# A one-core hybrid decoder trunk: SBUF slots picked by expected release, and store latency in the emission model

## The chip, the cores and the metric

The kernel runs on one core of one Trainium2 chip. The metric is the device time of one execution in microseconds; for the kernel before there are three timed runs, 1,869.14 to 1,875.14 us with a median of 1,870.52 us, and one profiled execution.

## The reference

One decoder layer over a 2,048 x 1,024 float32 input: a pre-norm mixer whose input projection is split into a causal pooling half and a complex-diagonal state-space half, an output projection with a residual add, a SwiGLU feed-forward block of width 2,816, and a final norm.

```python
def reference(x, ...):
    u = rmsnorm(h, norm_mix) @ w_in
    u_pool, u_ssm = u[..., :D_POOL], u[..., D_POOL:]
    y_pool = pool_mixer(u_pool, w_pool, pool_scale)
    y_ssm = ssm_mixer(u_ssm, lam_re, lam_im, log_dt, b_re, b_im, c_re, c_im, d_skip, w_glu, b_glu)
    h = h + concatenate([y_pool, y_ssm], axis=-1) @ w_out
    h = h + (silu(rmsnorm(h, norm_ffn) @ w_gate) * (rmsnorm(h, norm_ffn) @ w_up)) @ w_down
    return rmsnorm(h, norm_final)
```

## The kernel before

**The work.** Everything is held transposed: features in the 128 partitions, 512 tokens in the free dimension, so 2,048 tokens are four token blocks. A float32 product is made of three matmuls in the chip's fp32r type: each operand is split into a high part (ScalarE casts it, `act(hi, t)`) and a low part (VectorE subtracts the cast from the raw values), and the PE adds hi x hi, hi x lo and lo x hi in one PSUM bank. The stages follow each other: input projection, pooling and state-space work beside it, output projection, gate and up products, down products with the final norm. The gate and up products take the stretch from about 590 to 1,400 us, and every time in the text that falls there belongs to them.

**Gate and up products.** The product is cut into 2 x 2 blocks and made with seven block products instead of eight, named P1, P5, P6, P3, P7, P2, P4 in the order of `PR`. The loop runs over two pairs of token blocks (`hh`) and 11 pairs of feature blocks (`g`), so 22 groups; in each, `matrices` (line 1577) makes the seven products for gate and for up, 12 matmuls each. ScalarE copies some finished banks out to SBUF (line 1613, an eviction), VectorE adds others onto such copies; sigmoid, multiply and the block sums that the down stage will need follow, and `keep_ff` (line 1529) with `put` (line 1443) stores the seven results of a group to DRAM (`act..._P1` and so on), 256 KB each. `w_fetch` and `w_prep` (lines 1314, 1325) load the weights of later groups and split them. All DMAs are issued by SyncE from one queue, in order.

**Slots.** SBUF is cut by hand into slots of three sizes: 2 of 8 KB a partition (names b0, b1), 46 of 4 KB (s0 to s45) and 10 of 2 KB (t0 to t9). `Slots` (line 44) hands out a tag from a queue of free ones, always the one freed longest ago:

```python
        tag = self.free_ids.popleft()
```

`Units` (line 69) hands out 2 KB units. It takes a spare part of a large slot that it has already cut up, if there is one; else a t slot; else it cuts up a b slot into four (while `quads` is set) or an s slot into two:

```python
        if not self.spare[dt]:
            if self.small.left():
                return self.small(shape, dt)
            if self.quads and self.quad.left():
                pool, n = self.quad, 4
```

A slot is freed in the program's text when its last user has been emitted, not when that user has run. The first write to a slot's new tile therefore waits, by a semaphore, for all that still reads or writes the old one, a DMA that stores it included.

**The order of the work.** `Flow` (line 116) is a small model of the machine that runs while the program is written. It keeps a clock `now` for the PE, one each for VectorE, ScalarE, GpSimd and the DMA queue, and for each piece of a slot the time at which it was last written (`wrote`) and read (`read`). Streams of work beside the main one are generators; `poll` takes a step of each when the model's clocks say that its turn has come. So the model's times set the order on VectorE, ScalarE and SyncE, and the chip follows that order with its own times. In `dma` (line 206) a store marks its source as read at the time at which the transfer ends.

Of the kernel before, what the change touches and what calls it, by code (L numbers as in the profile page):

```python
# [29 lines left out]
KE = 8  # L30
MOST, KU, M0, M1, MD = 18, 8, 8, 12, 30
WL, WC = 7, 4
OP, RS = (2, 3), 12
HI, HK0, WPM, HF = (3, 2), 6, 5, 2
WAT, PF, TB, LK, BK = (3, 1), 3, 2, 1, 2
HK = "l"
# [7 lines left out]
class Slots:  # L44


    def __init__(self, pool, tag, n):
        self.pool, self.free_ids, self.of = pool, deque(f"{tag}{i}" for i in range(n)), {}
        self.count = 0

    def __call__(self, shape, dt=F32):
        if not self.free_ids:
            raise RuntimeError("no free slot")
        tag = self.free_ids.popleft()
        self.count += 1
        t = self.pool.tile(shape, dt, tag=tag, name=f"{tag}_{self.count}")
        self.of[id(t)] = (tag, t)
        return t
# [10 lines left out]
class Units:  # L69
# [9 lines left out]
                + (4 * self.quad.left() if self.quads else 0))  # L79

    def __call__(self, shape, dt=F32):
        if not self.spare[dt]:
            if self.small.left():
                return self.small(shape, dt)
            if self.quads and self.quad.left():
                pool, n = self.quad, 4
            elif self.used < self.most:
                pool, n = self.big, 2
                self.used += 1
            else:  # L90
                raise RuntimeError("no free unit")
            t = pool([128, n, 512], dt)
            self.spare[dt] += [(t, i, pool, n) for i in range(n)]
        part = self.spare[dt].pop(0)
        u = part[0][:, part[1], :]
        if len(shape) == 3:
            u = u.rearrange("p (a b) -> p a b", a=shape[1])
        self.of[id(u)] = (u, part, dt)
        return u
# [17 lines left out]
class Flow:  # L117
# [85 lines left out]
    def dma(self, dst, src):  # L203
        self.nc.sync.dma_start(dst, src)  # L204
        n = 4
        for d in dst.shape:
            n *= d
        us, ks = n / 3.5e5, self._keys(dst)
        self.t["d"] = max(self.t["d"], self.now) + us
        t = max([self.now, self.when(src)] + [self.read.get(k, 0.0) for k in ks]) + us  # L210
        self._end(max([t, self.t["d"]] + [self.wrote.get(k, 0.0) - 2.2 for k in ks]), 2.2, dst, [src])

    def read_of(self, ap):
        return max(self.read.get(k, 0.0) for k in self._keys(ap))
# [53 lines left out]
def hybrid_kernel(ctx: ExitStack, tc: tile.TileContext, x4, win, wpl, wglu, wout, wg, wu, wd, vecs, pinv,  # L268
# [6 lines left out]
    B, S = Slots(spool, "b", NB_), Slots(spool, "s", NS_)  # L275
    T = Units(Slots(spool, "t", NT_), S, B)
    PS = Slots(ppool, "p", 8)
    fl = Flow(nc)
    tt, ts, stt, cp, act, mm = fl.tt, fl.ts, fl.stt, fl.cp, fl.act, fl.mm

    def bank():
        return PS([128, 512])
# [683 lines left out]
    def main():  # L966
# [169 lines left out]
        def y_ssm(tb, keep=2):  # L1136
            while ssm[0] in fl.sides:
                yield fl.now + 0.5
            yield from room(2, keep)
            for i in (2, 3):  # L1140
                y_load(tb, i)
            for i in (2, 3):
                yield fl.when(yr[tb, i]) - 0.2
                yield from room(2, keep)
                y_split(tb, i)
            yield max(fl.t["v"], fl.t["a"]) + 0.5
            yield from glu(tb)
# [49 lines left out]
        def w_done(tb, m, ps):  # L1197
            fl.until(lambda: (tb, m // 2) in hin)
            hq = ht[tb, m // 2][:, m % 2, :]
            tt("v", hq, ps, hq, ADD)  # L1200
            PS.free(ps)
            h_sq(tb, m)
# [267 lines left out]
        for tb in range(4):  # L1470
            nxt = []
            for m in range(8):
                if (tb, m) == OP:
                    fl.side(ops_prep(0, 1))
                if tb < 3:
                    if m == 1:
                        nxt.append(fl.side(y_ssm(tb + 1)))
                    elif m == 4:
                        fl.side(h_in(tb + 1))
                elif m == 0:  # L1480
                    for i in range(2):
                        S.free(*gl[i])
                    T.most, res[0] = M0, 0
                elif m == WPM:
                    wp += [fl.side(w_fetch()), fl.side(w_prep())]
                fl.until(lambda: (1, m // 2) in wo)
                ps = bank()
                yield from w_part(tb, m, range(4 if (tb, m) in early else 0, 8), ps)
                w_done(tb, m, ps)
                if tb == 3 and m % 2:  # L1490
                    for half in range(2):
                        S.free(*wo.pop((half, m // 2), ()))
            for i in (2, 3):
                S.free(*yh.pop((tb, i)))
            if tb % 2 and (0, tb // 2) in ph:
                for g in range(4):
                    S.free(*ph.pop((g, tb // 2)))
            fl.side(h_finish(tb), HK if tb > 1 else "v")
            for n in nxt:
                fl.drain(n)  # L1500
# [430 lines left out]
```

## Time and profile before

| what | us |
|---|---|
| median of the three runs | 1,870.52 |
| the profiled execution's own time | 1,865.18 |
| its span, first to last instruction | 1,863.1 |
| PE busy in the span | 1,779.1 (95%) |
| VectorE busy | 1,331.9 (71%) |
| ScalarE busy | 711.6 (38%) |
| 16 DMA engines, the core's own queue | 50.8% of the span |
| mean granted clock of TensorE | 0.982 |

The PE row counts matmuls that overlap in the pipeline, so a busy PE says little of its rate; the number of matmuls in a stretch of fixed length says more. An engine that has less than all its time busy may still hold another one up at single places, and those places are found in the view of waits and in the timeline.

### The profile page before, as it was taken

How to read it: one execution, taken by the hardware profiler on the slowest of the kernel's cores; microseconds unless marked ns; L12 is line 12 of the kernel's file. 1: busy time of each engine (PE TensorE's matmuls, PEld its weight loads, DVE VectorE, ACT ScalarE, POOL GpSimd, SP SyncE). 2: the span in 40 equal slices, each digit the busy share in tenths (PEclk: the TensorE clock that was granted, in tenths of full speed). 3: DMA queues.
4: the chain of work that ended last, by engine and by line, in shares of the span. 5: the costliest groups of instructions: out<-in, count | busy, mean ns of one | idle time of the engine just before them, and what ended most of it. 6: DMA issues, size and time to landing. Idle time of an engine off the chain costs nothing.

```text
span 1863.1 us, 23354 instructions
## 1 busy us (share of the span) xinstructions
PE 1779.1 (95%) x8192; PEld 1453.6 (78%) x8192; DVE 1331.9 (71%) x2385; ACT 711.6 (38%) x1226; POOL 10.9 (1%) x29
## 2 busy tenths in 40 slices
PE   7999989899878899999999999999999999999997
PEld 6887767677767788787788887888778888888886
DVE  7979697657788667775778766777676556675666
ACT  5522333243243333332444333433244444454452
POOL 0000000000000000000000000000000000000000
PEclk9999999999999899999999999999999999999998
DMA  6461442474753444324644454443556666776653
GB/s 189 142 134 59 94 105 80 117 303 180 261 203 140 137 153 159 119 102 153 209 163 141 140 174 168 157 141 132 172 212 238 196 196 188 248 267 183 230 187 113
DMA packets 173093, 311.37 MB, mean 167 GB/s; under 512 B 25712, under 2 KB 52336, under 8 KB 172976
## 3 DMA queue, kind: packets, MB, share of 16 engines
q1 hardware_dynamic: 172976, 309.88, 50.8%
q8 instruction: 64, 1.05, 0.2%
q14 instruction: 53, 0.43, 0.1%
HBM read 210.59 MB, written 98.04 MB: 166 GB/s over the span
## 4 chain that ended last, share of the span: by engine, by line
PE 83%; DVE 7%; DMA 7%; SPq 2%; issue 1%; ACT 1%; DVEq 0%; ACTq 0%
PE p L189 83%; DVE s L166 3%; DMA act_P<-b 2%; SPq L204 2%; DMA act_P<-s 1%; DVE t L166 1%; DVE b L166 1%; DVE s L177 1%; DMA s<-in_win_dram 1%; DMA s<-hp 0%; DMA s<-in_wout_dram 0%; ACT b L185 0%; DMA hp<-s 0%; DMA ys<-b 0%; DMA s<-in_cst_dram 0%
## 5 line engine op out<-in xcount | busy, mean ns | idle before, releaser
L189 PE MATMUL p<-s,s 128*128 128x512 f32 (+3 forms) x5540 | 1386.6, 385 | 50.5 <-ACT s L185 25.2
L189 PEld LDWEIGHTS p<-s,s 128*128 128x128 f32 (+2 forms) x5540 | 989.9, 185 | 273.1 <-ACT s L185 28.2
L189 PE MATMUL p<-s,t 128*128 128x512 f32 (+1 forms) x1548 | 474.7, 387 | 8.7 <-DMA s<-in_wout_dram 4.2
L189 PEld LDWEIGHTS p<-s,t 128*128 128x128 f32 x1548 | 290.0, 190 | 69.5 <-issue 4.6
L166 DVE TENSOR_TENSOR s<-s,s 128x512 f32<-128x512 f32 (+5 forms) x299 | 261.8, 897 | 55.6 <-ACT s L185 36.6
L185 ACT ACTIVATE s<-b 128x512 fp32r<-128x512 f32 (+1 forms) x273 | 167.3, 629 | 229.3 <-PE p L189 166.1
L185 ACT ACTIVATE s<-s 128x512 fp32r<-128x512 f32 (+4 forms) x239 | 175.2, 746 | 144.8 <-DVE s L166 60.5
L166 DVE TENSOR_TENSOR s<-p,s 128x512 f32<-128x512 f32 (+3 forms) x209 | 134.1, 658 | 73.1 <-PE p L189 62.5
L185 ACT ACTIVATE b<-p 128x512 f32<-128x512 f32 (+1 forms) x105 | 61.2, 594 | 244.2 <-PE p L189 113.6
L166 DVE TENSOR_TENSOR s<-b,s 128x512 fp32r<-128x512 f32 (+1 forms) x166 | 113.2, 688 | 57.2 <-issue 30.1
L185 ACT ACTIVATE s<-p 128x512 f32<-128x512 f32 (+2 forms) x121 | 70.0, 591 | 188.5 <-PE p L189 86.2
L189 PE MATMUL p<-t,s 128*128 128x512 f32 (+1 forms) x292 | 108.6, 387 | 0.0
L166 DVE TENSOR_TENSOR t<-b,s 128x512 fp32r<-128x512 f32 (+1 forms) x125 | 85.7, 687 | 11.5 <-issue 4.7
L189 PE MATMUL p<-t,t 128*128 128x512 f32 x196 | 75.6, 389 | 0.0
L166 DVE TENSOR_TENSOR b<-p,b 128x512 f32<-128x512 f32 x94 | 64.6, 688 | 10.7 <-PE p L189 9.1
L166 DVE TENSOR_TENSOR s<-s,t 128x512 f32<-128x512 f32 (+1 forms) x55 | 37.8, 689 | 43.8 <-ACT t L185 26.5
L185 ACT ACTIVATE t<-s 128x512 fp32r<-128x512 f32 (+1 forms) x68 | 42.8, 632 | 68.9 <-DVE s L166 66.3
L166 DVE TENSOR_TENSOR s<-t,s 128x512 fp32r<-128x512 f32 (+2 forms) x71 | 47.7, 674 | 28.4 <-issue 21.9
L166 DVE TENSOR_TENSOR b<-b,b 128x512 f32<-128x512 f32 (+2 forms) x76 | 51.3, 676 | 23.3 <-DMA act_P<-b 12.4
L189 PEld LDWEIGHTS p<-t,s 128*128 128x128 f32 x292 | 54.9, 188 | 11.0
L166 DVE TENSOR_TENSOR s<-s,b 128x512 f32<-128x512 f32 x80 | 55.1, 689 | 11.6 <-DMA act_P<-s 6.4
L185 ACT ACTIVATE t<-b 128x512 fp32r<-128x512 f32 (+1 forms) x78 | 48.9, 627 | 36.4 <-DVE b L166 21.9
(105 smaller groups left out, 1052.5 us busy)
## 6 DMA issues: line engine op xcount, KB each, us to landing
act_P<-b SPq DMA_DIRECT2D x84, 256.0 KB, 5.0
b<-act_P SPq DMA_DIRECT2D x84, 256.0 KB, 3.5
s<-in_x_dram SPq DMA_DIRECT2D x40, 512.0 KB, 6.8
b<-ws_P SPq DMA_DIRECT2D x77, 256.0 KB, 2.8
act_P<-s SPq DMA_DIRECT2D x66, 256.0 KB, 5.1
b<-in_wd_dram SPq DMA_DIRECT2D x62, 256.0 KB, 3.2
t<-act_P SPq DMA_DIRECT2D x53, 256.0 KB, 3.4
s<-in_wu_dram SPq DMA_DIRECT2D x38, 256.0 KB, 3.3
```

Source lines behind the costliest of these rows:

```text
L166: self.eng(e).tensor_tensor(out, a, b, op=op)
L177: self.eng(e).scalar_tensor_tensor(out=out, in0=a, scalar=s, in1=b, op0=op0, op1=op1)
L185: self.nc.scalar.activation(out=out, in_=a, func=func, **kw)
L189: self.nc.tensor.matmul(out, l, r, start=start, stop=stop, skip_group_check=more)
L204: self.nc.sync.dma_start(dst, src)
```

## The change

Three things. `Slots` no longer takes the slot freed longest ago but the free slot for which the model expects the last reader or writer to be done soonest (`soonest`; among slots that are already done, all have the time `now`, and the one freed longest ago is taken). `Units` compares in the same way the spare parts, the t slots, and a large slot to be cut up, for which it adds 1.0 us; on equal times a t slot now comes ahead of a spare part. And a store marks its source as read `DS` = 3.0 us after the transfer's modelled end. The new constant `OK = "v"` is the value that `side` has by default, so that line does nothing.

```diff
--- before.py
+++ after.py
@@ -30,7 +30,8 @@
 KE = 8
 MOST, KU, M0, M1, MD = 18, 8, 8, 12, 30
 WL, WC = 7, 4
-OP, RS = (2, 3), 12
+OK = "v"
+OP, RS, DS = (2, 3), 12, 3.0
 HI, HK0, WPM, HF = (3, 2), 6, 5, 2
 WAT, PF, TB, LK, BK = (3, 1), 3, 2, 1, 2
 HK = "l"
@@ -47,11 +48,17 @@
     def __init__(self, pool, tag, n):
         self.pool, self.free_ids, self.of = pool, deque(f"{tag}{i}" for i in range(n)), {}
         self.count = 0
+        self.ready = lambda tag, chunks: 0.0
+
+    def soonest(self):
+        return min(((self.ready(t, range(4)), i) for i, t in enumerate(self.free_ids)), default=(1e9, 0))
 
     def __call__(self, shape, dt=F32):
         if not self.free_ids:
             raise RuntimeError("no free slot")
-        tag = self.free_ids.popleft()
+        i = self.soonest()[1]
+        tag = self.free_ids[i]
+        del self.free_ids[i]
         self.count += 1
         t = self.pool.tile(shape, dt, tag=tag, name=f"{tag}_{self.count}")
         self.of[id(t)] = (tag, t)
@@ -79,19 +86,22 @@
                 + (4 * self.quad.left() if self.quads else 0))
 
     def __call__(self, shape, dt=F32):
-        if not self.spare[dt]:
-            if self.small.left():
-                return self.small(shape, dt)
-            if self.quads and self.quad.left():
-                pool, n = self.quad, 4
-            elif self.used < self.most:
-                pool, n = self.big, 2
-                self.used += 1
-            else:
-                raise RuntimeError("no free unit")
+        spare = self.spare[dt]
+        old = min(((p[2].ready(p[2].of[id(p[0])][0], (p[1],)), i) for i, p in enumerate(spare)), default=(1e9, 0))
+        pool = self.quad if self.quads and self.quad.left() else self.big if self.used < self.most else None
+        new = pool.soonest()[0] + 1.0 if pool else 1e9
+        few = self.small.soonest()[0]
+        if min(old[0], few, new) == 1e9:
+            raise RuntimeError("no free unit")
+        if few <= min(old[0], new):
+            return self.small(shape, dt)
+        if new < old[0]:
+            n = 4 if pool is self.quad else 2
+            self.used += pool is self.big
             t = pool([128, n, 512], dt)
-            self.spare[dt] += [(t, i, pool, n) for i in range(n)]
-        part = self.spare[dt].pop(0)
+            old = (new, len(spare))
+            spare += [(t, i, pool, n) for i in range(n)]
+        part = spare.pop(old[1])
         u = part[0][:, part[1], :]
         if len(shape) == 3:
             u = u.rearrange("p (a b) -> p a b", a=shape[1])
@@ -208,7 +218,10 @@
         us, ks = n / 3.5e5, self._keys(dst)
         self.t["d"] = max(self.t["d"], self.now) + us
         t = max([self.now, self.when(src)] + [self.read.get(k, 0.0) for k in ks]) + us
-        self._end(max([t, self.t["d"]] + [self.wrote.get(k, 0.0) - 2.2 for k in ks]), 2.2, dst, [src])
+        t = max([t, self.t["d"]] + [self.wrote.get(k, 0.0) - 2.2 for k in ks])
+        self._end(t, 2.2, dst, [])
+        for k in self._keys(src):
+            self.read[k] = max(self.read.get(k, 0.0), t + DS)
 
     def read_of(self, ap):
         return max(self.read.get(k, 0.0) for k in self._keys(ap))
@@ -276,6 +289,8 @@
     T = Units(Slots(spool, "t", NT_), S, B)
     PS = Slots(ppool, "p", 8)
     fl = Flow(nc)
+    B.ready = S.ready = T.small.ready = lambda tag, chunks: max(
+        [fl.now] + [max(fl.read.get((tag, c), 0.0), fl.wrote.get((tag, c), 0.0)) for c in chunks])
     tt, ts, stt, cp, act, mm = fl.tt, fl.ts, fl.stt, fl.cp, fl.act, fl.mm
 
     def bank():
@@ -1471,7 +1486,7 @@
             nxt = []
             for m in range(8):
                 if (tb, m) == OP:
-                    fl.side(ops_prep(0, 1))
+                    fl.side(ops_prep(0, 1), OK)
                 if tb < 3:
                     if m == 1:
                         nxt.append(fl.side(y_ssm(tb + 1)))
```

The order of the matmuls on the PE stays as it was, but for four of them near the end (about 1,820 us) that move ahead of six others. On VectorE and ScalarE neighbours change places by a few rows between 582 and 1,400 us. What changes nearly everywhere is which slot an instruction writes to, and so what it waits for. In the rows below a name has the slot (b1), the number of its tile and a running number; p7 is a PSUM bank. The brackets name the semaphores waited for: DMAHW is a DMA's landing, the others are engines.

ScalarE, the end of the first gate and up group (about 600 to 612 us), before:

```order
L185 ACTIVATE t6_103_4982<-b0_5_4575 128x512 [waits DVE_49]
L185 ACTIVATE b1_7_4764<-p0_192_4971 128x512 [waits DVE_49,PE_49]
L185 ACTIVATE s45_351_4512<-p2_193_4994 128x512 [waits DMAHW1_49,DVE_49,PE_49]
L185 ACTIVATE s41_386_4911<-s19_377_4752 128x512
L185 ACTIVATE b1_7_4764<-p7_194_5014 128x512 [waits DMAHW1_49,DVE_49,PE_49]
```

and now:

```order
L195 ACTIVATE s32_381_4803<-b0_5_4576 128x512 [waits DVE_49]
L195 ACTIVATE t1_104_4993<-p0_192_4971 128x512 [waits PE_49,Activation_49]
L195 ACTIVATE t0_106_5015<-p2_193_4995 128x512 [waits PE_49]
L195 ACTIVATE s32_381_4803<-b1_8_4764 128x512 [waits DVE_49,Activation_49]
L195 ACTIVATE t6_108_5045<-p7_194_5017 128x512 [waits PE_49,Activation_49]
```

The last row is the same eviction, of bank p7. It went to a part of slot b1, behind a store out of it; now it goes to t6, whose last tile was an operand of matmuls, and no DMA semaphore is left in its wait. The eviction of p2 two rows above it has moved in the same way from s45 to t0.

ScalarE, the seventh group (about 845 to 853 us), before:

```order
L185 ACTIVATE s2_391_5157<-s30_406_6569 128x512 [waits DVE_49,PE_49]
L185 ACTIVATE s38_399_5840<-p0_228_6648 128x512 [waits DMAHW0_49,DVE_49,PE_49]
L185 ACTIVATE s13_393_5407<-s33_402_6180 128x512
L185 ACTIVATE b1_7_4764<-p2_229_6684 128x512 [waits DMAHW1_49,DVE_49,PE_49]
L185 ACTIVATE s30_406_6569<-p7_230_6703 128x512 [waits DMAHW7_49,DVE_49,PE_49]
```

and now:

```order
L195 ACTIVATE s24_437_6764<-p2_229_6744 128x512 [waits PE_49]
L195 ACTIVATE s0_432_6575<-s6_428_6483 128x512 [waits DVE_49]
L195 ACTIVATE t1_216_6781<-t2_209_6571 128x512 [waits DMAHW6_49]
L195 ACTIVATE s33_440_6792<-b0_5_4576 128x512 [waits DMAHW7_49]
L195 ACTIVATE t4_218_6796<-p7_230_6766 128x512 [waits PE_49]
```

The eviction of bank p7 in the last row went to slot s30 behind a store, and now goes to t4 and waits for the PE alone. Of the rows ahead of it some casts have changed places.

SyncE, the loads near 740 us, before:

```order
L204 DMA bsP7_1_3566<-t9_151_5836 128x512 [waits DMAHW0_49,DVE_49]
L204 DMA bsP4_1_3568<-s38_399_5840 128x512 [waits DMAHW1_49,DVE_49]
L204 DMA t6_161_6113<-in_wg_dram 128x512 [waits DMAHW2_49,Activation_49]
L204 DMA t9_162_6115<-in_wu_dram 128x512 [waits DMAHW3_49,DMAHW0_49]
L204 DMA s38_399_5840<-bn2_1_124 128x512 [waits DMAHW4_49,DVE_49]
L204 DMA t2_164_6122<-bn3_1_128 128x512 [waits DMAHW5_49,PE_49]
L204 DMA t1_165_6124<-bn3_3_130 128x512 [waits DMAHW6_49,PE_49]
```

and now:

```order
L214 DMA t1_175_6005<-in_wg_dram 128x512 [waits DMAHW0_49,PE_49]
L214 DMA s4_413_5887<-in_wu_dram 128x512 [waits DMAHW3_49,DMAHW1_49]
L214 DMA t3_183_6153<-in_wg_dram 128x512 [waits DMAHW2_49,DVE_49,PE_49]
L214 DMA b0_5_4576<-in_wu_dram 128x512 [waits DVE_49]
L214 DMA s4_413_5887<-bn2_1_124 128x512 [waits DMAHW4_49,DVE_49]
L214 DMA s0_419_6161<-bn3_1_128 128x512 [waits DMAHW5_49]
L214 DMA s0_419_6161<-bn3_3_130 128x512 [waits DMAHW6_49]
```

The third row is the same weight load. It went to t6, which waited for ScalarE, and now goes to t3, which waits for VectorE and the PE; the row behind it waits for VectorE, and the loads of the normed activations (bn) follow.

## Rows read from the trace of the kernel before

**Rows 1.** The page's first line: the span.

```profile
span 1863.1 us, 23354 instructions
```

**Rows 2.** The chain that ended last, share of the span by line (page, part 4).

```profile
PE p L189 83%; DVE s L166 3%; DMA act_P<-b 2%; SPq L204 2%; DMA act_P<-s 1%; DVE t L166 1%; DVE b L166 1%; DVE s L177 1%; DMA s<-in_win_dram 1%; DMA s<-hp 0%; DMA s<-in_wout_dram 0%; ACT b L185 0%; DMA hp<-s 0%; DMA ys<-b 0%; DMA s<-in_cst_dram 0%
```

**Rows 3.** Windows of 50 us: busy time (instructions) by engine, PEclk, DMA share, GB/s.

```profile
600.00:650.00 50.00, 43.74 (x181) 35.58 (x180) 30.73 (x49) 16.27 (x29) 0.00 (x0) 0.90 0.39 128
650.00:700.00 50.00, 50.00 (x222) 41.42 (x221) 32.04 (x52) 18.52 (x34) 0.00 (x0) 1.00 0.50 165
...
750.00:800.00 50.00, 47.38 (x203) 38.72 (x202) 36.62 (x60) 17.07 (x30) 0.00 (x0) 0.97 0.39 129
...
850.00:900.00 50.00, 45.74 (x193) 36.71 (x192) 32.19 (x52) 18.15 (x34) 0.00 (x0) 0.97 0.48 163
...
1150.00:1200.00 50.00, 49.14 (x217) 40.38 (x216) 31.08 (x50) 15.12 (x27) 0.00 (x0) 1.00 0.58 195
1200.00:1250.00 50.00, 49.15 (x218) 40.35 (x217) 35.92 (x58) 19.73 (x36) 0.00 (x0) 1.00 0.45 152
...
1300.00:1350.00 50.00, 48.53 (x215) 39.86 (x214) 31.09 (x51) 14.26 (x25) 0.00 (x0) 1.00 0.51 167
1350.00:1400.00 50.00, 48.46 (x213) 39.54 (x212) 34.11 (x54) 20.28 (x36) 0.00 (x0) 1.00 0.60 215
```

**Rows 4.** Waits, 590 to 1,400 us: us in total, times, longest.

```profile
ACT b L185 <- DMA act_P<-b: 97.0, 18, 10.4
DVE b L166 <- DMA act_P<-b: 81.3, 20, 6.5
ACT s L185 <- DVE b L166: 70.2, 43, 6.8
...
ACT s L185 <- DMA act_P<-s: 52.2, 9, 8.1
...
PE p L189 <- ACT s L185: 11.3, 4, 6.3
...
PE p L189 <- ACT b L185: 6.5, 4, 2.6
```

**Rows 5.** Waits of the PE, 200 to 590 us.

```profile
PE p L189 <- DVE s L166: 18.5, 9, 4.6
PE p L189 <- DVE b L166: 7.4, 3, 3.7
```

**Rows 6.** Timeline, 599 to 613 us: start, us, engine, line, op, [idle before <-releaser].

```profile
599.99 0.69 DVE L166 TENSOR_TENSOR t<-b,s 128x512 f32<-128x512 f32 x1
...
605.88 0.39 PE L189 MATMUL p<-s,t 128*128 128x512 f32 x1
...
606.03 0.42 SPq L204 DMA_DIRECT2D act_P<-b  x1
...
611.35 0.60 ACT L185 ACTIVATE b<-p 128x512 f32<-128x512 f32 x1 [9.97 <-DMA act_P<-b]
...
612.52 0.79 PE L189 MATMUL p<-s,s 128*128 128x512 f32 x1 [6.26 <-ACT s L185]
```

**Rows 7.** DMA issues (page, part 6): times, KB each, median us to landing.

```profile
act_P<-b SPq DMA_DIRECT2D x84, 256.0 KB, 5.0
...
act_P<-s SPq DMA_DIRECT2D x66, 256.0 KB, 5.1
...
s<-in_wu_dram SPq DMA_DIRECT2D x38, 256.0 KB, 3.3
```

**Rows 8.** Timeline near 740 us: a weight load, a matmul group, the casts of that weight.

```profile
740.91 0.38 SPq L204 DMA_DIRECT2D t<-in_wg_dram  x1
...
753.98 0.84 PE L189 MATMUL p<-s,s 128*128 128x512 f32 x3
...
776.34 1.14 ACT L185 ACTIVATE s<-t 128x512 fp32r<-128x512 f32 x2
```

**Rows 9.** The down stage as one window, columns as in rows 3.

```profile
1400.00:1850.00 450.00, 447.48 (x2038) 372.26 (x2036) 286.70 (x506) 203.12 (x355) 1.79 (x3) 1.00 0.63 206
```

## The prediction

> **What bounds the kernel now.** The chain of work that ended last lies on the PE for 83% of the span [rows 1, 2]. Behind it come stores to the buffers of the gate and up products (act_P, 2% and 1%), each about as long in the chain as VectorE's largest line. A store ends nothing by itself, so it can stand in such a chain only where somebody waits for the memory it reads from. I then read the windows of 50 us. The PE is busy nearly all the time in each, but the number of matmuls tells its rate: a window that runs undisturbed has 222, and of the sixteen from 600 to 1,400 us seven have clearly fewer [rows 3]. The down stage behind is busy for 447.48 of 450 us [rows 9], so it has little to give.
>
> Next the waits. From 590 to 1,400 us the PE waits for ScalarE alone, 11.3 and 6.5 us in eight places, and ScalarE waits 97.0 and 52.2 us for the landing of stores [rows 4]. The two are one chain, and the timeline of the longest place shows it [rows 6]. VectorE has read the old contents of a slot by 600.68 us (599.99 + 0.69). The store out of that slot is issued only at 606.03 us, behind other DMAs in SyncE's queue. ScalarE, which is to evict a finished bank into the same slot, starts at 611.35 us after 9.97 us idle. Behind it stands the cast that the PE needs. The PE, whose last matmul began at 605.88 us, goes on at 612.52 us after 6.26 us idle.
>
> Before 590 us the PE waits mostly for VectorE's results, 18.5 and 7.4 us [rows 5]. Those are operands not yet made, with VectorE at work until the moment it delivers them; no store and no slot stands behind them.
>
> **The change, part by part.**
>
> *Slots picked by expected release.* The change adds and removes no instruction. It moves the evictions at the eight places away from slots behind a fresh store. At the first place the eviction of bank p7 now goes to t6, and in the seventh group to t4: both slots held operands of matmuls, the ScalarE rows have no DMA semaphore left in their wait, and the bank itself is finished by those same or later matmuls. So the new wait costs nothing: the eviction has to wait for that bank anyhow. The others of the eight go the same way: seven now go to slots that matmuls read last, and one to a slot whose store landed some 40 us earlier. I carried the same check over all instructions of the stretch: with the end times of the trace before, no ScalarE or VectorE instruction of the changed order waits for a recent store. What goes is therefore all of ScalarE's 97.0 and 52.2 us and VectorE's 81.3 us [rows 4], nearly all of it idle time that cost nothing, and with it the eight waits of the PE.
>
> What the eight are worth I take from the windows, since a pause also leaves the clock at its lower level (1.2 instead of 2.4 GHz) for a while: PEclk is 0.90 and twice 0.97 where the longest pauses lie, and 1.00 elsewhere [rows 3]. The windows with 181, 203, 193, 217, 218, 215 and 213 matmuls lack 41, 19, 29, 5, 4, 7 and 9 against 222: 114 in all. At 50 / 222 = 0.225 us each that is **25.7 us**. The waits alone make 11.3 + 6.5 = 17.8 us [rows 4]; the remaining 7.9 us are matmuls at the lower clock and the restart after each pause. So 17.8 us is the lower bound if the clock comes back no better, and 25.7 us the value I take, because the clock rows show the loss in the same windows as the pauses.
>
> Would the next limit stand right behind? At the first place ScalarE was free from 601.4 us and the PE asked at about 606.3 us, so some 5 us lie between, and the operands that follow are made by engines that are idle today: VectorE is busy 30.73 of 50 us there, ScalarE 16.27 [rows 3].
>
> *The store's latency.* The model used to call a store's source free when the transfer ends, 256 KB / 3.5e5 = 0.75 us after its start. Now it adds 3.0 us, 3.75 in all. The trace has 5.0 and 5.1 us from issue to landing [rows 7], so the model is still about 1.3 us short. If each of the eight evictions took a slot at that edge, 8 x 1.3 = 10.4 us would come back; none does, so I take zero. The Trainium skill (DMA: Bandwidth & Descriptors, Anatomy of one DMA) gives a fixed 2.0 us plus bytes at 436e3 per us. By that an estimate for 256 KB is 2.6 us, the model would count too much, and the sum would be the same 25.7 us. The rows differ from that page, and they decide.
>
> *Order and units.* The shifts by a few rows on VectorE and ScalarE add waits of ScalarE for VectorE's last read of a slot. Such waits are today 70.2 us in 43 places without the PE noticing [rows 4], and VectorE, freed of its own 81.3 us, will be earlier. I take zero; the bounds are a gain of nothing and a loss as large as one place of the eight, 25.7 / 8 = 3.2 us.
>
> *SyncE's queue.* Some weight loads now go to slots that matmuls still read. The load issued at 740.91 us would wait in its new slot t3 for a matmul group that ends at about 754.1 us, 13 us later, with the loads and stores behind it in the queue. Its casts run at 776.34 us [rows 8]. A load takes 3.3 us [rows 7], so 754.1 + 3.3 leaves 19 us: zero.
>
> *The sum.* 1,865.2 - 25.7 = **1,839.5 us** for the profiled execution. The median of the runs before is 1,870.52, which is 5.3 us above the profiled one. I carry this over and predict **1,845 us** for the median.
>
> **The rivals.**
>
> *The latency is still counted too short.* Then slots are handed out 1.3 us before the store lands, and 10.4 us come back: 1,845 + 10.4 = 1,855 us. The 5.0 us of the rows speak for it, the absent DMA semaphores in the evictions against. 12%.
>
> *There are too few slots, whichever is picked.* Every slot is then behind some store or reader, the waits only change their names, and the time stays at 1,870 us. This is also the case in which the change does not do what it says. The Trainium skill (Perfetto Trace Analysis, Optimization Strategy) reads the same gap repeated on the engine that should be saturated as a sign that SBUF may be too small for the next tile. The trace agrees as to the gap: it comes back in seven windows [rows 3]. Against the rest of it speaks that the evictions do find slots without a store. 4%.
>
> *The head of SyncE's queue.* All DMAs stand in one queue, so a load that waits for a matmul holds up the stores and loads behind it. It decides when such a load is more than 32 us late (776.3 - 740.9 - 3.3): then the cast waits, ScalarE works in order, and the evictions behind the cast leave the PE without a bank. One such stall costs what one of the eight does, 3.2 us; with one in each of 22 groups, 70 us, and the time is 1,845 + 70 = 1,915 us. From the tenth stall on it is slower than before. For it: the wait of 13 us above. Against: the 19 us that are left. 4%.
>
> **How the numbers follow.** Forecast 80%, the rivals 12, 4 and 4%. A measurement of this kernel can tell about 0.3%, 5.6 us, from no change. Forecast and first rival lie below 1,865, so faster has 0.92, the same 0.04 and slower 0.04. The range goes from 1,838 us (the 1,839.5 of the profiled execution, should the 5.3 us above it not come back, and a little more) to 1,855 us (the first rival; the lower bound of 17.8 us, which gives 1,853, lies inside).
>
> **What would show it.** Right: in the profile after, ScalarE and VectorE have hardly a wait for act_P from 590 to 1,400 us, the PE's waits of 17.8 us there are nearly gone, all sixteen windows have 213 or more matmuls and most 220 to 223, PEclk is 1.00 in them, and the stretch before 590 us looks as it did. The latency rival would show as waits for act_P of 1 to 2 us; the second as waits of old length under other names; the third as casts that wait for weight loads and long waits at the head of SyncE's queue. The prediction is wrong if the gate and up windows are full and the total still stays above 1,855 us, because then the time has gone to another stage.

## The result, and the profile after

The changed kernel takes 1,839.26 us (median; 1,837.82 to 1,842.11 us). The kernel before, run beside it, takes 1,869.94 us (1,869.14 to 1,875.14 us). The ratio is 0.9832, with a 95% interval of 0.981 to 0.9854. Four executions among the comparisons of this study (one of the kernel before, three of edited kernels) took 3,569 to 6,312 us, about twice to three and a half times the rest, and are left out of all ratios and counts. The prediction was 1,845 us with a range of 1,838 to 1,855 us, so the direction and the range hold; the point lies 5.7 us too high, and the result is near the lower end of the range.

The head of the page of the changed kernel, to be read beside [rows 1] and [rows 2]:

```profile
span 1837.1 us, 23226 instructions
...
PE 1770.6 (96%) x8192; PEld 1450.0 (79%) x8192; DVE 1341.1 (73%) x2385; ACT 717.7 (39%) x1226; POOL 10.9 (1%) x29
...
PE 91%; DVE 5%; DMA 2%; SPq 1%; issue 1%; ACT 0%; DVEq 0%; ACTq 0%
PE p L199 91%; DVE s L176 3%; SPq L214 1%; DVE s L187 1%; DMA s<-in_win_dram 1%; DVE t L176 1%; DMA s<-in_wout_dram 0%; DMA s<-in_cst_dram 0%; DMA ys<-b 0%; DMA s<-ys 0%; PE p L203 0%; DVE nwt L176 0%; DVE b L176 0%; ACT s L195 0%; ACT t L195 0%
```

The span is 26.0 us shorter, with the same work (every engine has the same number of working instructions as before; the 128 fewer in the total are others, such as waits). The stores of the gate and up products have left the chain of work that ended last; the PE is 91% of it, 83% before. (All line numbers of the helpers are 10 higher than before: line 199 is the matmul, 195 ScalarE, 176 VectorE, 214 the DMAs.)

Windows of 50 us of the changed kernel, columns as in [rows 3]:

```profile
600.00:650.00 50.00, 50.00 (x223) 41.39 (x222) 39.18 (x64) 22.57 (x41) 0.00 (x0) 1.00 0.55 195
...
750.00:800.00 50.00, 50.00 (x222) 41.42 (x221) 33.93 (x54) 19.50 (x35) 0.00 (x0) 1.00 0.51 177
...
850.00:900.00 50.00, 50.00 (x223) 41.39 (x221) 38.77 (x61) 17.65 (x31) 0.00 (x0) 1.00 0.42 143
...
1350.00:1400.00 50.00, 50.00 (x222) 41.41 (x221) 34.03 (x55) 19.89 (x36) 0.00 (x0) 1.00 0.44 156
```

These are four of sixteen; each of the sixteen has 222 or 223 matmuls and a PEclk (the granted share of TensorE's full clock) of 1.00. In the windows where the kernel before had 181, 203, 193 and 213, nothing is missing any more. The stretch from 600 to 1,400 us as one window gives the best measure of the gain. The PE's columns (us, PE busy, matmuls, PEclk, DMA share, GB/s), of the kernel before:

```profile
600.00:1400.00 800.00, 782.13 (x3411) 0.99 0.46 155
```

and of the changed kernel:

```profile
600.00:1400.00 800.00, 800.00 (x3531) 1.00 0.46 162
```

A matmul of an undisturbed stretch takes 800 / 3,531 = 0.2266 us. The 120 that were missing make 120 x 0.2266 = 27.2 us. That is the whole gain and a little more: the PE's last pause ahead of this stretch, with 2,631 matmuls ahead of it in both traces, now ends at 577.79 us, before at 576.11 us, so the profiled execution after is 1.7 us late there. It falls behind in the first 200 us. The kernel before:

```profile
0.00:200.00 200.00, 188.46 (x931) 1.00 0.48 131
```

and the changed kernel:

```profile
0.00:200.00 200.00, 187.89 (x924) 0.99 0.48 130
```

This is no effect of the change: the second trace of the same changed kernel (the change again, below) has 930 matmuls there, and all the traces of this study have 914 to 931, with a granted clock of 0.98 to 1.00.

Waits from 590 to 1,400 us in the changed kernel (us in total, times, longest), a choice of lines:

```profile
ACT t L195 <- PE p L199: 155.0, 100, 3.5
...
DVE t L176 <- DMA act_P<-t: 4.9, 4, 2.1
ACT b L195 <- DMA b<-act_P: 4.8, 1, 4.8
...
ACT t L195 <- DMA act_P<-t: 0.8, 1, 0.8
```

The PE has no row at all in this view; before, it had 17.8 us [rows 4]. ScalarE's 97.0 and 52.2 us behind stores are 0.8 us now, VectorE's 81.3 us are 4.9 us. A line of the kernel before that the prediction didn't count, VectorE behind stores out of 4 KB slots, has gone as well:

```profile
DVE s L166 <- DMA act_P<-s: 19.7, 5, 5.1
```

ScalarE still idles a lot, but now for the PE to finish a bank, which is what an engine that isn't the bound should wait for. The timeline at the first place, of the changed kernel (start, us, engine, line, operation, idle before):

```profile
602.64 0.60 ACT L195 ACTIVATE t<-p 128x512 f32<-128x512 f32 x1 [1.66 <-PE p L199]
...
604.88 0.39 PE L199 MATMUL p<-s,t 128*128 128x512 f32 x1
...
605.11 2.88 PE L199 MATMUL p<-s,s 128*128 128x512 f32 x12
...
607.83 2.88 PE L199 MATMUL p<-s,t 128*128 128x512 f32 x12
```

This is the eviction of bank p7 that started at 611.35 us after 9.97 us behind a store [rows 6]. It goes to t6 now, starts at 602.64 us, and has waited only for the bank. The PE runs through the place where it stood for 6.26 us.

The PE's waits in the stretch before are nearly the same. Waits of the PE from 200 to 590 us, of the changed kernel, to be read beside [rows 5]:

```profile
PE p L199 <- DVE s L176: 20.1, 11, 4.5
PE p L199 <- DVE b L176: 7.4, 3, 3.7
```

### The profile page after: what moved, and what is told of

Same layout as the page of the kernel before. It is cut to its first block, busy times and chain, and to the rows that moved or that the text cites. A ratio compares the mean times of both kernels' runs of the same rounds, so it can differ in the third digit from the quotient of the medians.

```text
span 1837.1 us, 23226 instructions
## 1 busy us (share of the span) xinstructions
PE 1770.6 (96%) x8192; PEld 1450.0 (79%) x8192; DVE 1341.1 (73%) x2385; ACT 717.7 (39%) x1226; POOL 10.9 (1%) x29
## 4 chain that ended last, share of the span: by engine, by line
PE 91%; DVE 5%; DMA 2%; SPq 1%; issue 1%; ACT 0%; DVEq 0%; ACTq 0%
PE p L199 91%; DVE s L176 3%; SPq L214 1%; DVE s L187 1%; DMA s<-in_win_dram 1%; DVE t L176 1%; DMA s<-in_wout_dram 0%; DMA s<-in_cst_dram 0%; DMA ys<-b 0%; DMA s<-ys 0%; PE p L203 0%; DVE nwt L176 0%; DVE b L176 0%; ACT s L195 0%; ACT t L195 0%
## 5 line engine op out<-in xcount | busy, mean ns | idle before, releaser
L199 PE MATMUL p<-s,s 128*128 128x512 f32 (+4 forms) x4736 | 1188.7, 385 | 37.9 <-DVE s L176 21.8
L199 PEld LDWEIGHTS p<-s,s 128*128 128x128 f32 (+2 forms) x4736 | 840.5, 185 | 227.6 <-DVE s L176 25.5
L199 PE MATMUL p<-s,b 128*128 128x512 f32 x1000 | 319.6, 392 | 7.4 <-DVE b L176 7.4
L199 PEld LDWEIGHTS p<-s,b 128*128 128x128 f32 x1000 | 188.6, 189 | 47.8 <-DVE b L176 8.7
L195 ACT ACTIVATE s<-t 128x512 fp32r<-128x512 f32 (+1 forms) x174 | 105.3, 624 | 113.3 <-PE p L199 76.7
L195 ACT ACTIVATE t<-s 128x512 fp32r<-128x512 f32 (+2 forms) x129 | 78.5, 616 | 163.9 <-DVE s L176 148.6
L199 PE MATMUL p<-b,s 128*128 128x512 f32 (+2 forms) x476 | 132.6, 390 | 4.1 <-DMA s<-s 4.1
L176 DVE TENSOR_TENSOR t<-p,t 128x512 f32<-128x512 f32 x130 | 88.6, 689 | 39.5 <-PE p L199 35.8
L199 PEld LDWEIGHTS p<-b,s 128*128 128x128 f32 (+1 forms) x476 | 73.9, 176 | 25.7 <-issue 9.8
L176 DVE TENSOR_TENSOR t<-t,t 128x512 f32<-128x512 f32 (+2 forms) x121 | 81.7, 675 | 7.9 <-ACT t L195 6.5
```

The costliest lines, as they stand in the source:

```text
L176: self.eng(e).tensor_tensor(out, a, b, op=op)
L195: self.nc.scalar.activation(out=out, in_=a, func=func, **kw)
L199: self.nc.tensor.matmul(out, l, r, start=start, stop=stop, skip_group_check=more)
```

## The experiments

Eleven kernels. The first four and the complement (units alone) take the change apart; one moves the latency the other way; one runs the change again; two take slots away; two eat into the margin of SyncE's queue. All are edits of the changed kernel unless it says otherwise. The table has the profiled execution's time, the ratio to the kernel before on the same chip, and the matmuls from 600 to 1,400 us. "Worked out" is 1,838.88 us (the profiled execution of the change) plus 0.2266 us for each matmul short of 3,531.

| kernel | us | ratio (95%) | matmuls | worked out |
|---|---|---|---|---|
| before | 1,865.18 | 1 | 3,411 | 1,866.1 |
| the change | 1,838.88 | 0.9832 (0.981 to 0.9854) | 3,531 | 1,838.9 |
| no latency | 1,842.46 | 0.9857 (0.9833 to 0.988) | 3,524 | 1,840.5 |
| latency only | 1,870.01 | 1.0008 (0.9993 to 1.0022) | 3,408 | 1,866.8 |
| preference only | 1,884.49 | 1.009 (1.0072 to 1.0107) | 3,333 | 1,883.7 |
| old order of units | 1,873.07 | 1.0025 (1.0013 to 1.0037) | 3,387 | 1,871.5 |
| latency of 6 us | 1,841.27 | 0.9855 (0.9825 to 0.9885) | 3,531 | 1,838.9 |
| eight t slots | 1,840.52 | 0.9854 (0.9837 to 0.9872) | 3,531 | 1,838.9 |
| units alone | 1,839.67 | 0.985 (0.9829 to 0.987) | 3,532 | 1,838.7 |
| the change again | 1,839.77 | 0.9855 (0.9838 to 0.9873) | 3,531 | 1,838.9 |
| loads later | 1,839.91 | 0.9835 (0.9816 to 0.9854) | 3,531 | 1,838.9 |
| loads latest | 1,863.10 | 0.997 (0.9956 to 0.9984) | 3,435 | 1,860.6 |
| less room | 1,863.78 | 0.9953 (0.9939 to 0.9967) | 3,480 | 1,850.4 |

In all rows but the last the two times agree within 4 us: most of what these kernels differ by in time lies from 600 to 1,400 us.

**No latency.**

```diff
-OP, RS, DS = (2, 3), 12, 3.0
+OP, RS, DS = (2, 3), 12, 0.0
```

> The changed kernel with DS = 0: slots are picked by expected release, but a store's source counts as free when the modelled transfer ends, 0.75 us after its start. My theory (what cost time was evictions put into slots whose store was still far from landing, and any choice by release avoids most of that): with the end times of the changed kernel's trace carried over the new order, ScalarE has nine waits for a store of more than 1 us between 590 and 1,400 us, the longest 4.2 us, where the kernel before has more than twenty with several of 6 to 9 us. At the longest place of before, ScalarE's idle time of 9.97 us became 6.26 us at the PE, so some 3.7 us were spare there: waits of up to 4.2 us cost the PE nearly nothing. So 1,839 to 1,844 us. Rival (the latency is what does it, without it the choice is blind to stores): the time goes back to 1,860 us or more. Third theory (both matter about equally): about 1,850 to 1,855 us.

As my theory had it. The PE has one wait left in the stretch, at the first place. Its timeline in this kernel:

```profile
607.00 0.69 DVE L176 TENSOR_TENSOR t<-t,t 128x512 f32<-128x512 f32 x1 [4.21 <-DMA act_P<-t]
...
608.35 1.88 PE L199 MATMUL p<-s,s 128*128 128x512 f32 x7 [1.48 <-DVE s L176]
```

So a slot with a fresh store is picked here, VectorE waits 4.21 us for it, and 1.48 us of that reach the PE; the window lacks seven matmuls, 1.6 us. That is all that the latency is worth in this stretch. Whether it is worth it in the total can't be told: the intervals of this kernel and of the change overlap.

**Latency only** (edits of the kernel before).

```diff
-        self._end(max([t, self.t["d"]] + [self.wrote.get(k, 0.0) - 2.2 for k in ks]), 2.2, dst, [src])
+        t = max([t, self.t["d"]] + [self.wrote.get(k, 0.0) - 2.2 for k in ks])
+        self._end(t, 2.2, dst, [])
+        for k in self._keys(src):
+            self.read[k] = max(self.read.get(k, 0.0), t + DS)
```

> The kernel before with the store's latency alone (the source of a store counts as read 3.0 us after the modelled transfer), slots still handed out in the order in which they were freed. My theory: the choice is blind to the model's times, so evictions go on landing in slots behind fresh stores (carried over, ScalarE has some 30 waits for a store of more than 1 us, ten of them over 5 us); the time stays at 1,864 to 1,876 us, and the windows from 600 to 1,400 us keep a loss of some 100 matmuls. Rival (the latency moves the order of ScalarE's and VectorE's work, since streams wait for reads in the model, and that order is the gain): 1,840 us.

No difference from the kernel before. Waits of ScalarE and VectorE from 590 to 1,400 us in this kernel:

```profile
ACT b L185 <- DMA act_P<-b: 71.7, 12, 11.0
...
DVE b L166 <- DMA act_P<-b: 55.6, 13, 7.4
ACT s L185 <- DMA act_P<-s: 54.6, 15, 6.5
```

The model knows of the stores now, but the queue of free slots doesn't ask it. The order on ScalarE and VectorE does move, and gains nothing by it.

**Preference only.**

```diff
-    B.ready = S.ready = T.small.ready = lambda tag, chunks: max(
-        [fl.now] + [max(fl.read.get((tag, c), 0.0), fl.wrote.get((tag, c), 0.0)) for c in chunks])
```

> The changed kernel with all expected releases read as zero: what stays is the new order of preference in the units (a t slot ahead of a spare part of a large slot) and the latency. My theory: without the times the t slots go to evictions and store results in the order in which they were freed, and waits for stores come back (carried over: 25 of ScalarE over 1 us, 15 of them over 5 us); 1,862 to 1,880 us. Rival (the gain is that evictions now take t slots in place of parts of the two big slots, whatever the time of release): 1,839 to 1,845 us.

Slower than before, and 3.8 us above the upper end I gave (median 1,883.79 us). Waits from 590 to 1,400 us in this kernel:

```profile
DVE t L176 <- DMA act_P<-t: 135.9, 34, 10.8
ACT t L195 <- DMA act_P<-t: 57.2, 15, 9.0
```

and the timeline of its longest pause in the middle of the stretch:

```profile
995.38 0.42 SPq L214 DMA_DIRECT2D act_P<-t  x1
...
1001.32 0.69 DVE L176 TENSOR_TENSOR t<-b,t 128x512 fp32r<-128x512 f32 x1 [7.61 <-DMA act_P<-t]
...
1002.07 1.22 PE L199 MATMUL p<-s,t 128*128 128x512 f32 x2 [6.04 <-DVE t L176]
```

Ten t slots that are always taken first come round quickly, so they come round behind their own stores. The last such store ahead of the wait is the one issued at 995.38 us. What is held up here is a low part that VectorE is to write, and VectorE's results hold the PE for 23.7 of its 28.9 us of waits in the stretch. My count had looked at ScalarE alone, which is likely why it was too small.

**Old order of units.** The choice in `Units` as before, `Slots` and the latency as changed:

```diff
-        spare = self.spare[dt]
-        old = min(((p[2].ready(p[2].of[id(p[0])][0], (p[1],)), i) for i, p in enumerate(spare)), default=(1e9, 0))
...
+        if not self.spare[dt]:
+            if self.small.left():
+                return self.small(shape, dt)
...
+        part = self.spare[dt].pop(0)
```

> The changed kernel with the choice in the units as before (spare part first, then a t slot, then a large slot cut up), while the slots of each size are still picked by expected release and the latency counts. My theory: at seven of the eight places of the kernel before the eviction went to a spare part of a large slot, and a spare part freed behind a store is taken first here as well, so the waits stay (carried over: 31 of ScalarE over 1 us, 14 of them over 5 us): 1,862 to 1,885 us. Rival (the choice among slots of one size is enough): 1,839 to 1,845 us.

The gain is gone. The timeline of the first place in this kernel (its helpers' lines are three lower than in the changed kernel, 192 ScalarE and 196 the matmul):

```profile
615.82 0.60 ACT L192 ACTIVATE b<-p 128x512 f32<-128x512 f32 x1 [10.90 <-DMA act_P<-b]
...
616.99 1.22 PE L196 MATMUL p<-s,t 128*128 128x512 f32 x2 [7.68 <-ACT t L192]
```

It is the picture of [rows 6] once more, 1.4 us longer at the PE: an eviction into a part of a large slot behind that slot's store.

**Units alone.** The complement: slots of 8 and 4 KB in the order of freeing, only the units choose.

```diff
+        l = list(self.free_ids)[:1] if self.tag in "bs" else self.free_ids
-        return min(((self.ready(t, range(4)), i) for i, t in enumerate(self.free_ids)), default=(1e9, 0))
+        return min(((self.ready(t, range(4)), i) for i, t in enumerate(l)), default=(1e9, 0))
```

> The changed kernel with the slots of 8 KB and 4 KB handed out in the order of freeing again; the choice by release stays among the t slots and between t slots, spare parts and large slots. It is the complement of the run with the old order of the units. My theory: the evictions that held the PE up take units, so the whole gain lies in the choice of units; the order of work on every engine is that of the changed kernel, and carried over ScalarE has two waits for stores, 1.4 us in all: 1,836 to 1,844 us. Rival (the choice among large slots carries part of it): 1,848 us or more.

The whole gain. With the run before this one it settles which part of the change works: the choice in `Units` by the expected release, among spare parts, t slots and a new large slot. The choice among slots of one large size did nothing here. Whether the comparison between the kinds is needed, or a choice among the spare parts alone would do, isn't separated: the old order took both away.

**Latency of 6 us.**

```diff
-OP, RS, DS = (2, 3), 12, 3.0
+OP, RS, DS = (2, 3), 12, 6.0
```

> The changed kernel with DS = 6.0 in place of 3.0, so that the model's 6.75 us from the start of a store lie above every median of landing in the trace of before (5.0 and 5.1 us). My theory: the choice with 3.0 avoids the stores already, all windows from 600 to 1,400 us have 222 or 223 matmuls, and there is nothing left to gain: the same as the changed kernel, 1,836 to 1,843 us. Rival (the latency is still counted short and costs somewhere): faster than the changed kernel by 3 us or more.

No gain: the stretch is full at 3.0 already.

**The change again**, with no edit.

> The changed kernel once more, for a comparison on the same chip with the others of this group and for the term of 5.3 us that the prediction carried over from the runs of before. If the profiled execution of before was a fast one by chance, the median here lies within 2 us of the profiled execution, as in the first runs (1,839.26 against 1,838.88 us): 1,836 to 1,843 us. Rival (kernels of this kind take about 5 us more without the profiler): median 1,843 us or more, 4 to 6 us above the profiled execution.

The median is 1,839.77 us and the profiled execution took the same. This kernel has no surcharge on runs beside the profiled one.

**Eight t slots.**

```diff
-NB_, NS_, NT_ = 2, 46, 10
+NB_, NS_, NT_ = 2, 46, 8
```

> The changed kernel with eight t slots in place of ten. It tells how much room the choice needs. My theory: slots without a fresh store are plentiful, so the choice still finds one (carried over, ScalarE has no wait for a store of more than 0.7 us): 1,837 to 1,846 us. Rival (the slots are just enough, and the gain hangs on having ten): waits for stores or readers come back under other names, 1,850 us or more.

As fast as with ten.

**Less room.**

```diff
-NB_, NS_, NT_ = 2, 46, 10
+NB_, NS_, NT_ = 2, 42, 8
```

> The changed kernel with 42 slots of 4 KB in place of 46 and eight t slots in place of ten, 20 KB a partition less. Where the run with eight t slots takes away units alone, this one takes room from every stage; the order on the PE moves too (454 matmuls, all by at most 64 places). My theory: the choice still finds slots without a fresh store from 600 to 1,400 us (carried over, five waits of ScalarE for a store of over 1 us, the longest 3.5 us), but with fewer free slots the evictions wait more for readers, and the input side of the kernel, where I have checked nothing, may lose some too: 1,838 to 1,856 us. Rival (room was scarce all the time, and the choice by release only helped as long as it had 56 slots): 1,860 us or more.

The median is 1,859.33 us, 3.3 us above my range and just short of the rival's. Against the change its profiled execution takes 24.9 us more. The matmuls from 600 to 1,400 us explain 51 x 0.2266 = 11.6 us of it. The rest lies earlier. The window from 400 to 600 us of the PE in this kernel,

```profile
400.00:600.00 200.00, 172.86 (x727) 0.94 0.57 208
```

and in the changed kernel:

```profile
400.00:600.00 200.00, 176.62 (x755) 0.94 0.55 200
```

That is 28 matmuls or 6.3 us less, and from 0 to 400 us another 32 are missing (1,942 against 1,974), 7.3 us. Part of that is scatter: the other kernels with all the slots of the change and its choice have 1,964 to 1,974 matmuls up to 400 us. The PE's waits from 590 to 1,400 us in the kernel with less room name VectorE alone:

```profile
PE p L199 <- DVE s L176: 6.7, 5, 2.3
PE p L199 <- DVE b L176: 1.2, 2, 1.0
PE p L199 <- DVE t L176: 0.9, 1, 0.9
```

VectorE itself waits only 6.9 us for the products' stores there, little more than the 4.9 us of the change. Half of the 51 matmuls are missing in the first window:

```profile
600.00:650.00 50.00, 47.59 (x197) 0.95 0.27 97
```

Three more windows lack 4, 16 and 7 against 222 (from 850 to 950 and from 1,300 to 1,350 us), the others are full, and nothing more is lost after 1,400 us, since the losses up to there (11.6, 6.3 and 7.3 us) already make up the 24.9 us. So a kernel with 50 of these slots loses time that one with 54 doesn't, up to about 650 us and at a few places behind, and what the PE waits for in the stretch are operands that VectorE delivers later. What makes VectorE later there wasn't traced further, and the order on the PE moved too, so room and order aren't separated.

**Loads later.**

```diff
-WL, WC = 7, 4
+WL, WC = 4, 4
```

> The changed kernel with the weights loaded at most 4 products ahead in place of 7 (WL = 4). In the changed kernel the DMA at the head of SyncE's queue waits 210.7 us in 28 places for matmuls between 590 and 1,400 us, 21.1 us the longest, against 20.2 us in 16 places before; the prediction gave a load about 32 us until its cast is late, 19 us of them left at the place it looked at. A product takes about 36.8 / 7 = 5.3 us (22 groups in 810 us), so loads come some 16 us later. My theory (the queue has that margin): 3 us of the 19 are left, at most a few short pauses: 1,838 to 1,850 us. Rival (the waits at the head of the queue have used the margin up): casts wait for loads in most of the 22 groups, 3.2 us each, up to 1,839 + 70 = 1,909 us.

No loss: no wait of the PE in the stretch, 3,531 matmuls. The loads do come later: by the trace they are issued 16 us (median) further on in the PE's work than in the changed kernel.

**Loads latest.** The same line with `WL = 2`.

> The same with WL = 2: loads come 5 products or 26 us later than in the changed kernel, more than the 19 us that were left at the place of the prediction, but less than the 32 us from a load's start to its cast. My theory: now the casts are late by some 7 us and pauses come back; with 3.2 us in each of 22 groups up to 70 us, 1,860 to 1,910 us. Rival (even 26 us less does not matter): 1,845 us or less. Third theory (the third rival of the prediction was priced too low): above 1,910 us.

The median is 1,863.75 us, inside my range, but the mechanism is not the one I had described. The loads are issued 28 us (median) further on in the PE's work, and yet ScalarE waits only 2.1 us for a weight load in the stretch. What has gone is the lead of the work on the weights: `w_prep` can't cast a weight before `w_fetch` has emitted its load, so `WL = 2` also holds the casts below the four products that `WC` allows. Some waits of ScalarE for the products' stores are back as well. Waits from 590 to 1,400 us in this kernel:

```profile
PE p L199 <- DVE b L176: 4.1, 7, 1.7
PE p L199 <- ACT t L195: 2.5, 4, 1.2
...
ACT t L195 <- DMA act_P<-t: 17.7, 12, 2.5
```

A place in the timeline of this kernel:

```profile
1231.74 0.63 ACT L195 ACTIVATE t<-t 128x512 fp32r<-128x512 f32 x1 [2.17 <-DMA act_P<-t]
...
1232.41 0.69 DVE L176 TENSOR_TENSOR b<-t,t 128x512 fp32r<-128x512 f32 x1 [2.61 <-ACT t L195]
...
1232.43 0.73 PE L199 MATMUL p<-s,t 128*128 128x512 f32 x2 [0.77 <-ACT t L195]
```

Cast, low part and matmul start within 0.7 us of each other, so a small delay, here a cast that stood behind a store for 2.17 us, reaches the PE. How much of the loss is the lost lead and how much the stores wasn't separated. Two windows of the PE in this kernel show the result:

```profile
1200.00:1250.00 50.00, 49.09 (x214) 1.00 0.38 132
...
1350.00:1400.00 50.00, 48.55 (x209) 1.00 0.60 221
```

All sixteen windows lack some matmuls, 2 to 13 of 222, and the granted clock stays at 1.00. This is a thin loss everywhere, where the kernel before had eight pauses.

## Why the prediction was right, and where it was off

*What bounds the kernel, and the eight places.* Right. The eight pauses are gone, and with them ScalarE's and VectorE's waits for the products' stores. The experiments show the cause: wherever evictions and low parts go to slots behind fresh stores (latency only, preference only, old order of units), 123 to 198 matmuls are missing, and where the choice in `Units` avoids most of that, none or seven, unless room or the lead of the loads is cut far down.

*The price, 25.7 us.* Right for the profiled executions: 1,865.18 - 1,838.88 = 26.3 us. The one long window gives 27.2 us: an undisturbed window has 222 or 223 matmuls, 222.4 in the mean of the sixteen after the change, and I had counted all against 222. That the forecast for the profiled execution came within 0.6 us is partly luck, because the 1.5 us by which the price is short of 27.2 us are about the 1.7 us that the execution after was late by its first 200 us. The lower bound of 17.8 us (the PE's waits alone) was 9 us short. So the pauses did cost about half as much again as they lasted, as the windows' matmuls said. Where the extra half lies can be read from [rows 3]: the three windows with a granted clock of 0.90 and 0.97 lack 89 matmuls, 20.0 us, while the PE is idle for 13.1 us; the four with 1.00 lack 25, 5.6 us, with 4.7 us idle. So nearly all of it is in the windows where the clock fell.

*The carry-over of 5.3 us.* This step failed, and it is the only one that moved the number. I took the distance between the profiled execution before and the median for a property of the kernel that the change would keep. Over all comparisons of this study the kernel before has 52 times with a median of 1,868.0 us, from 1,860.9 to 1,875.1 us; 6 of them lie at or below the profiled 1,865.18 us. The changed kernel has eight, from 1,837.8 to 1,842.1 us. The profiled execution before was a low draw from a wide scatter, the one after an ordinary one from a narrow one. Eight times say little of how narrow, though: 26 executions of seven kernels without long pauses (the change twice, no latency, latency of 6 us, eight t slots, units alone, loads later) go from 1,835.5 to 1,843.5 us. Nor does the scatter belong to the pauses alone: loads latest, which has no long pause, spreads over 8.3 us in ten executions, and latency only, which has them, over 8.0 us in ten. It does go with the granted clock. Of the 48 executions before for which the mean clock is on record, the five with 0.983 took 1,860.9 to 1,865.9 us, the three with 0.978 took 1,871.5 to 1,874.5 us. A part lies outside the gate and up stretch: the profiled execution before had 931 matmuls in its first 200 us, the most of any trace here. What makes the clock differ between executions stays open.

*The latency.* Right that 3.0 us suffices, wrong in the weight I gave it. The first rival priced a latency that is 1.3 us short at 10.4 us. With no latency at all only seven matmuls are missing, 1.6 us, and with 6.0 us none are gained. A likely reason, not tried by itself, lies in the rule: among the slots that the model takes for done, the one freed longest ago comes first, so one whose store is still under way is seldom next.

*Too few slots.* This rival did not come true, and two t slots less cost nothing. Six slots less do cost some 20 us, but VectorE's and ScalarE's waits for the products' stores stay at 6.9 and 4.2 us there, so it isn't the rival as I had described it. The sign that the Trainium skill names (Perfetto Trace Analysis, Optimization Strategy: the same gap coming back can mean that there isn't enough SBUF for the next tile) was there in the trace before. Here the slots were enough, and the handing out was wrong.

*SyncE's queue.* The cost of zero was right and the wait that I had found was not a single one. The DMA at the head of the queue waits for matmuls, from 590 to 1,400 us in the changed kernel,

```profile
SPq L214 <- PE p L199: 210.7, 28, 21.1
```

and in the kernel before:

```profile
SPq L204 <- PE p L189: 20.2, 16, 5.1
```

Ten times as much, up to 21.1 us where I had worked out 13. But the head of the queue doesn't wait longer in all: every row of that view together makes 588 us before and 590 us now, because the waits for VectorE fell from 510 to 361 us. Loads that come some 16 us later still cost nothing, and some 28 us later they cost 21.8 us (96 matmuls). So the queue has at least those 16 us. Where its margin ends the second run doesn't tell, since what ends there is the lead of the work on the weights, not a cast that waits for a load; and the stalls that the rival priced at 70 us did not appear.

*Order, and waits of VectorE.* The zero for the moved rows holds: the PE waits for nobody in the stretch. I expected no wait of VectorE for a recent store; four are left for the products' stores, 4.9 us in all, which the PE doesn't notice.

## What to carry to other kernels

Where slots are handed out by hand, look in the waits for engines that wait for a store whose data they don't need: that is a slot reused too soon, and taking a finished slot beside it cost nothing here. The comparison that brought the gain here crosses the kinds of slots (a part of a large slot against a small one), while choosing by release among the large slots of one size brought nothing; a fixed preference for one kind without the times was worse than none. And price a pause by the matmuls that are missing from a stretch, not by the wait alone.

## What the runs showed of the hardware that I had not expected

The stores became faster. DMA issues of the changed kernel (times, KB each, median us to landing), against 5.0 and 5.1 us before [rows 7]:

```profile
act_P<-t SPq DMA_DIRECT2D x84, 256.0 KB, 2.5
...
act_P<-s SPq DMA_DIRECT2D x52, 256.0 KB, 3.9
```

I sorted the products' stores from 590 to 1,400 us by how many DMAs of the queue had been issued and had not landed yet when the store was issued, from the issue and landing times of the traces:

| DMAs in flight | before: stores, median us | after: stores, median us |
|---|---|---|
| 0 | 2, 2.01 | 13, 2.02 |
| 1 | 7, 2.31 | 18, 2.33 |
| 2 | 19, 2.51 | 42, 2.49 |
| 3 | 16, 3.69 | 11, 2.80 |
| 4 | 36, 5.07 | 15, 3.94 |
| 5 or more | 67, 5.47 | 53, 5.56 |

The same 256 KB take 2.0 us alone and 5.5 us behind five or more others. Before, 103 of 147 stores had four or more ahead of them; after the change it is 68 of 152. The estimate of 2.6 us that the prediction drew from the Trainium skill (DMA: Bandwidth & Descriptors, Anatomy of one DMA) comes from a formula that the page gives for DMAs issued by GpSimd, while SyncE issues these. It is above the 2.0 us of a store alone, near what one or two in flight give (2.3 and 2.5 us), and half of what a crowded queue gives. The 5.0 us of the rows before, which I had set against it, are the time of a crowded queue. That fewer in flight made the stores land sooner is what the sorting suggests; no run changed that number alone, and it isn't the whole of it, for with three or four in flight the stores after still land about 1 us sooner than before.
